# Gate rows by chunk and head on partitions, and the mLSTM units at other places in the order of the mixer stage

## The chip, the cores and the metric

The kernel runs on one core of a Trainium2 chip. The metric is the device time of one execution in microseconds (us). Three executions of the kernel before gave 1381.76, 1384.97 and 1388.18 us; the median is 1384.97 us. The profile belongs to one further execution.

Five engines work side by side, each through its own list of instructions, in order: PE multiplies matrices, DVE (VectorE) and ACT (ScalarE) work on tiles, POOL (GpSimd) is a third such engine, and SP issues DMA transfers. An instruction that waits holds up everything behind it on its engine, and nothing on the others unless they wait for it.

## The reference

The reference is one layer of a hybrid encoder over a prompt of 1024 frames and a running stream of 32 frames with a past of 256. The width is 1024. An adaptive norm modulates the input, one projection `w_in` feeds three groups of heads (mLSTM, forgetting attention "FoX", gMLP), one projection `w_o` joins them, then a norm, a SwiGLU FFN and a second norm follow. What the change touches is the gates:

```python
li = mi + b_mlstm_i                              # mLSTM input gate, 4 heads
lf = log_sigmoid(mf + b_mlstm_f)                 # mLSTM forget gate, 4 heads
logf = log_sigmoid(ff + b_fox_f)                 # FoX forget gate, 8 heads
# FoX: logits += F[t] - F[s],  F = cumsum(logf) over all frames
# mLSTM, chunk by chunk:
b = cumsum(lf)                                   # inside a chunk
m = maximum(m0 + b, max over s <= t of (b[t] - b[s] + li[s]))
m0_next = m[last]                                # and w = exp(... - m), d0 = exp(m0 + b[last] - m[last])
```

So the gates need cumulative sums over time, a running maximum of `li - b` inside each chunk, and a short recurrence over the chunks for the stabiliser `m0`. The kernel takes chunks of 128 frames: eight of the prompt and a ninth for the stream.

## The kernel before, in words

All matrices are split into a high and a low part of a reduced float32 type, so each step of a product is three matmuls: L117, L118 and L119 for products with features on partitions, L282, L283 and L284 for those with time on partitions (the stream's tile has L287, L288 and L290). A weight tile is loaded raw, ACT rounds it to its high part (L105), and DVE, or POOL where the order says so, subtracts to get the low part (L106). Every product's result comes in one of three PSUM banks `g`; transposes and small products share two banks `t`, attention scores two banks `s`, attention outputs one.

The stages are: the input and its modulation, the value projections (`tm_unit` v0 and v1, which also bring the gate columns), `gates()` (L424), then the mixer stage that the string `ORDER` lists, then the first four gMLP units and two key units, then `wo` (from 383 us in the profile), the norm, and the FFN with the rest of the mixers.

A token of `ORDER` is a unit: `q0` to `q7` the query and key product of a FoX head (`head_unit`, 24 matmuls of 512 columns; heads 0 and 1 have 48 more of 272 columns), `f0` to `f7` the attention of a head over the first 512 frames, in four tiles of 128 rows, `k0` and `k1` the key products of the mLSTM (a `p` puts L106 on POOL), `s` its states, `v` and `o` its value and output-gate products, `m0` to `m3` its first four chunks, and `a` one unit of the adaptive norm's modulation. An `a` unit loads two tiles `ada_late` of 512 KB, multiplies each in four matmuls (L179), has ACT copy the result, transposes it twice (L185), and DVE reduces it (L187).

The string isn't the final order. The program is built under a scheduler that simulates the engines with its own durations and writes a fixed list for each engine; units `f` and `m` are named with high priority. So a matmul of a later unit can fill a place at which the scheduler expects a wait. On the chip the lists are fixed: PE waits where its next instruction isn't ready. DMA transfers of SP are issued in its list's order, and a transfer that waits for its source or for a free tile holds those behind it.

`gates()` of before puts the four mLSTM heads and eight FoX heads in rows. It writes the gate columns into two tiles `gs` and `gl` of 96 columns a chunk, and for each of nine chunks multiplies by a triangle of ones (L464) and by the identity (L465), which gives `rb`: 96 rows (most of them empty) by nine chunks by 128 frames. The maximum is seven DVE steps over 4 rows by up to 1143 columns (L492), with POOL copying the start of each chunk (L493). The recurrence is three DVE steps a chunk (L504 to L506). FoX's cumulative sums get their carry (L471) and are split a chunk at a time (L475 to L478) and stored to DRAM `dfs`, from where `head_unit` loads four rows into `q2` and `k2`. Nine transposes of 128 by 128 (L530) and three DVE copies (L531) bring the results to columns `col`. The maximum goes to DRAM `dM`, from where each mLSTM chunk loads it, repeated over all partitions, into `mb`; DVE reads it in L585, the first step of a chunk.

A FoX tile's way is: two matmuls into a score bank (L752, L753), on DVE the mask on the diagonal (L755) and the row maximum (L756), on ACT the exponential (L761), on DVE the reciprocal (L765) and the scaling (L769), then transposes on PE (L788), a split on ACT and DVE (L794), and the products with the values (L796 to L805).

## Time and profile before

| what | before |
|---|---|
| median of the runs | 1384.97 us |
| profiled execution | 1386.62 us |
| its span, from first to last instruction | 1384.6 us |
| granted TensorE clock, mean | 0.99 |
| end of the value projections, PE | 106.95 us |
| `gates()` on PE | from 119.17 to 155.5 us |
| first attention score | 161.98 us |
| first matmul of `wo` | 383.24 us |

In the profile a row of a timeline gives the start and the duration of an instruction or of a group of like ones (`x8`), its engine, line and operation, the tiles out and in, and in brackets the idle time of that engine just before and what ended it. A row of windows gives for a stretch of time each engine's busy time, the TensorE clock that was granted (1.00 is full), the busy share of the DMA engines and GB/s. Matmuls overlap, so the time between the starts of two neighbours, and not their duration, is what one costs.

### The profile page before, as it was taken

How to read it: one execution, taken by the hardware profiler on the slowest of the kernel's cores; microseconds unless marked ns; L12 is line 12 of the kernel's file. 1: busy time of each engine (PE TensorE's matmuls, PEld its weight loads, DVE VectorE, ACT ScalarE, POOL GpSimd, SP SyncE). 2: the span in 40 equal slices, each digit the busy share in tenths (PEclk: the TensorE clock that was granted, in tenths of full speed). 3: DMA queues.
4: the chain of work that ended last, by engine and by line, in shares of the span. 5: the costliest groups of instructions: out<-in, count | busy, mean ns of one | idle time of the engine just before them, and what ended most of it. 6: DMA issues, size and time to landing. Idle time of an engine off the chain costs nothing.

```text
span 1384.6 us, 25402 instructions
## 1 busy us (share of the span) xinstructions
PE 1343.1 (97%) x9459; PEld 1226.1 (89%) x9459; DVE 1031.2 (74%) x2190; ACT 655.5 (47%) x1281; POOL 244.8 (18%) x276
## 2 busy tenths in 40 slices
PE   7999999999999899999999999999999999999996
PEld 4799788989899778888887889899999999999996
DVE  5547774678778757777776766678898988888777
ACT  3313354554545544545544455335564454545355
POOL 0102100042157500000000000264610000000341
PEclk9999999999999999999999999999999999999998
DMA  9763475455764765544444343564596768453321
GB/s 359 248 222 103 138 238 165 133 166 155 251 194 145 204 197 154 142 140 120 135 120 95 108 119 94 189 175 130 157 241 183 211 161 218 133 175 116 101 90 65
DMA packets 126386, 224.67 MB, mean 162 GB/s; under 512 B 21284, under 2 KB 70060, under 8 KB 126264
## 3 DMA queue, kind: packets, MB, share of 16 engines
q1 hardware_dynamic: 120952, 212.95, 49.4%
q0 software_dynamic: 5168, 9.96, 4.8%
q8 instruction: 75, 1.23, 0.4%
q14 instruction: 47, 0.39, 0.1%
q10 hardware_dynamic: 144, 0.14, 0.0%
HBM read 191.21 MB, written 51.72 MB: 175 GB/s over the span
## 4 chain that ended last, share of the span: by engine, by line
PE 83%; DVE 9%; DMA 4%; ACT 2%; issue 2%; POOL 1%; SPq 0%; DVEq 0%; ACTq 0%; POOLq 0%
PE up_g L117 5%; PE up_g L118 5%; PE up_g L119 5%; PE dn_g L119 4%; PE dn_g L117 4%; PE dn_g L118 4%; PE tm_g L282 3%; PE tm_g L283 3%; PE tm_g L284 3%; PE sup_u L119 3%; PE sup_u L117 3%; PE sup_u L118 3%; PE wo_g L118 2%; PE wo_g L119 2%; PE wo_g L117 2%; PE fox_t L788 2%
## 5 line engine op out<-in xcount | busy, mean ns | idle before, releaser
L117 PE MATMUL up_g<-mlstm_ah,up_whi 128*128 128x512 f32 (+1 forms) x384 | 141.3, 368 | 4.2 <-ACT lna_tmp L1037 3.4
L118 PE MATMUL up_g<-mlstm_al,up_whi 128*128 128x512 f32 (+1 forms) x384 | 141.5, 369 | 0.6 <-DVE mlstm_al L1042 0.6
L119 PE MATMUL up_g<-mlstm_ah,up_wlo 128*128 128x512 f32 (+1 forms) x384 | 140.7, 367 | 0.0
L283 PE MATMUL tm_g<-tm_wlo,start_h1h 128*128 128x256 f32 (+1 forms) x384 | 109.8, 287 | 0.0
L282 PE MATMUL tm_g<-tm_whi,start_h1h 128*128 128x256 f32 (+1 forms) x384 | 109.3, 287 | 0.0
L284 PE MATMUL tm_g<-tm_whi,start_h1l 128*128 128x256 f32 (+1 forms) x384 | 108.8, 285 | 0.0
L1161 ACT CAST sup_whi<-sup_raw 128x1024 fp32r<-128x1024 f32 x54 | 56.0, 1047 | 90.8 <-PE dn_u L118 47.4
L117 PEld LDWEIGHTS up_g<-mlstm_ah,up_whi 128*128 128x128 f32 x384 | 73.2, 191 | 16.9 <-ACT mlstm_ah L1041 3.6
L761 ACT ACTIVATE fox_p<-fox_s,fox_fmx 128x384 f32<-128x384 f32 (+2 forms) x96 | 55.2, 578 | 60.6 <-DVE fox_fmx L759 44.3
L118 PEld LDWEIGHTS up_g<-mlstm_al,up_whi 128*128 128x128 f32 x384 | 73.1, 190 | 11.9 <-DVE mlstm_al L1042 1.2
L119 PEld LDWEIGHTS up_g<-mlstm_ah,up_wlo 128*128 128x128 f32 x384 | 73.2, 191 | 10.6
L105 ACT CAST up_whi<-up_raw 128x1024 fp32r<-128x1024 f32 x50 | 52.4, 1048 | 61.6 <-PE up_g L118 18.2
L106 DVE TENSOR_TENSOR up_wlo<-up_raw,up_whi 128x1024 fp32r<-128x1024 f32 x50 | 66.8, 1336 | 14.0 <-ACT up_whi L105 13.3
L1016 DVE SCALAR_TENSOR_TENSOR wo_z<-dn_g,start_mod,wo_z 128x512 f32<-128x512 f32 (+4 forms) x120 | 60.2, 520 | 21.5 <-PE dn_g L119 19.6
L1162 DVE TENSOR_TENSOR sup_wlo<-sup_raw,sup_whi 128x1024 fp32r<-128x1024 f32 x54 | 68.1, 1264 | 10.5 <-ACT sup_whi L1161 10.5
L283 PEld LDWEIGHTS tm_g<-tm_wlo,start_h1h 128*128 128x128 f32 x384 | 72.3, 188 | 2.3 <-issue 2.1
L282 PEld LDWEIGHTS tm_g<-tm_whi,start_h1h 128*128 128x128 f32 x384 | 72.1, 189 | 1.7 <-issue 0.8
L117 PE MATMUL dn_g<-up_acth,dn_whi 128*128 128x512 f32 (+2 forms) x200 | 73.5, 368 | 0.0
L118 PE MATMUL dn_g<-up_actl,dn_whi 128*128 128x512 f32 (+2 forms) x200 | 73.4, 368 | 0.0
L119 PE MATMUL dn_g<-up_acth,dn_wlo 128*128 128x512 f32 (+2 forms) x200 | 73.3, 366 | 0.0
L284 PEld LDWEIGHTS tm_g<-tm_whi,start_h1l 128*128 128x128 f32 x384 | 72.2, 188 | 0.1
L117 PE MATMUL fm_g<-start_h1h,fm_whi 128*128 128x272 f32 (+2 forms) x200 | 60.6, 312 | 5.9 <-DVE fm_qkl L367 2.0
(628 smaller groups left out, 4628.9 us busy)
## 6 DMA issues: line engine op xcount, KB each, us to landing
up_raw<-w_gu SPq DMA_DIRECT2D x50, 512.0 KB
dn_raw<-w_dn SPq DMA_DIRECT2D x28, 512.0 KB
ada_late<-w_ada SPq DMA_DIRECT2D x24, 512.0 KB
wo_raw<-w_o SPq DMA_DIRECT2D x24, 512.0 KB
sup_raw<-w_gu SPq DMA_DIRECT2D x20, 512.0 KB
start_dp<-w_gu SPq DMA_DIRECT2D x19, 512.0 KB
start_dp<-w_gu POOLq DMA_DIRECT2D x19, 512.0 KB, 7.8
sup_raw<-start_dp SPq DMA_DIRECT2D x18, 512.0 KB
```

The source lines that it names most:

```text
L105: nc.scalar.copy(hi[:, :w], raw[:, :w])
L106: (eng or nc.vector).tensor_tensor(lo[:, :w], raw[:, :w], f(hi[:, :w]), ALU.subtract)
L117: nc.tensor.matmul(ps, hi, xh(k), start=start and k == 0, stop=False)
L118: nc.tensor.matmul(ps, hi, xl(k), start=False, stop=False)
L119: nc.tensor.matmul(ps, lo, xh(k), start=False, stop=stop and k == n - 1)
L282: nc.tensor.matmul(ps[:, :ncol], xh, hi, start=k == 0, stop=False)
L283: nc.tensor.matmul(ps[:, :ncol], xh, lo, start=False, stop=False)
L284: nc.tensor.matmul(ps[:, :ncol], xl, hi, start=False, stop=k == 7)
L761: nc.scalar.activation(pr[:, lo:hi], banks[x][:, :hi - lo], AF.Exp, bias=mxs[:, 0:1], accum_out=sums[:, x:x + 1])
L1016: self.lastz = self.nc.vector.scalar_tensor_tensor(z[:, m, x:y], ps[:, x - a:y - a], g[i], z[:, m, x:y], ALU.mult, ALU.add)
L1161: nc.scalar.copy(h, x)
L1162: tt(l, x, f(h), ALU.subtract)
```

## The change

Gates: a row is now a pair of chunk and head. The four gate tables are 36 or 72 columns wide, so one matmul for the FoX rows and three for the mLSTM rows replace the 18 of before. The maximum takes seven steps over 36 rows by 128 columns, shifted by a pad on the left. The carry of FoX's sums over the chunks is one small matmul with a matrix `ut` that POOL builds, and its split is done for all 64 rows at once; it is stored to `dfs` in two pieces. For the recurrence, the last column of each row is spread by a product with an indicator, one small matmul (`sel`) brings it to 4 heads by 18, eight DVE steps of 4 by 1 run the recurrence, and a second small matmul (`back`) brings `m0` and `m` back to the 36 rows. Four transposes of 36 rows and one copy give `col`. The pool of these tiles is on the other side of SBUF. `dfs` and `dM` have the new row order, so `decay()` loads four rows of `q2` or `k2` as four pieces of 512 bytes, and `mb` is one contiguous row of 2 KB for each partition.

Order: the mLSTM's key units, states and `v` come behind heads 0 and 1, `o` behind head 2, and chunks `m0` to `m3` in turns with heads 2 to 5.

```diff
-ORDER = "k0 k1p q0 f0 q1 a f1 s a q2 f2 a q3 f3 a v q4 f4 a q5 f5 o a m0 q6 f6 a m1 q7 m2 f7 a m3"
+ORDER = "q0 f0 q1 a f1 k0 k1p s a v q2 f2 a o a m0 q3 f3 a m1 q4 f4 a m2 q5 f5 a m3 q6 f6 a q7 f7"
...
+    def decay(self, out, h, rows, tiles):
+        j0, j1 = tiles
+        self.load(f(out).rearrange("p (j q) -> p j q", q=P),
+                  self.dfs.rearrange("(j h) r q -> h r j q", h=8)[h, rows, j0:j1])
...
-        self.load(f(q2[64:68]), self.dfs[h, 2:6, :512])
-        self.load(f(k2[64:68]), self.dfs[h, 0:4, :512])
+        self.decay(q2[64:68], h, slice(2, 6), (0, 4))
+        self.decay(k2[64:68], h, slice(0, 4), (0, 4))
...
-            for j in range(nj):
-                o = ps[:96, j * P:(j + 1) * P]
-                nc.tensor.matmul(o, gs[:, j0 + j, :], self.tri, start=True, stop=False)
-                nc.tensor.matmul(o, gl[:, j0 + j, :], self.ident, start=False, stop=True)
-            nc.scalar.copy(rb[:, j0:j0 + nj, :].rearrange("p j q -> p (j q)"), ps[:96, :nj * P])
...
+        ps = self.t(self.pt, [P, 512], F32, "t")
+        nc.tensor.matmul(ps[:72, 256:384], flat(gf), self.tri, start=True, stop=True)
+        nc.tensor.matmul(ps[:R, 0:128], flat(gn), self.tri, start=True, stop=False)
+        nc.tensor.matmul(ps[:R, 0:128], flat(gi), self.ident, start=False, stop=True)
+        nc.tensor.matmul(ps[:R, 128:256], flat(gm), self.tri, start=True, stop=True)
...
+        nc.tensor.matmul(pc[:64, 0:1], ut, rf[:64, P - 1:P], start=True, stop=True)
...
-            nc.vector.tensor_tensor(dst[:, :, w:], src[:, :, w:], src[:, :, :P - w], ALU.max)
-            nc.gpsimd.tensor_copy(dst[:, :, :w], src[:, :, :w])
...
+            nc.vector.tensor_tensor(v[:, 64:], u[:, 64:], u[:, w:w + P], ALU.max)
...
+        nc.tensor.matmul(pc[:4, 32:50], sel, EI.rearrange("p a j -> p (a j)"), start=True, stop=True)
+        ab = t([4, 2, 9], "ab")
+        nc.vector.tensor_copy(ab, pc[:4, 32:50].rearrange("p (a j) -> p a j", a=2))
         for j in range(8):
...
+            nc.vector.scalar_tensor_tensor(m0[:, j + 1:j + 2], ab[:, 0, j:j + 1], m0[:, j:j + 1], ab[:, 1, j:j + 1],
+                                           ALU.max, ALU.add)
+        nc.vector.tensor_copy(mm[:, 0, 0:8], m0[:, 0:8])
+        nc.vector.tensor_tensor(mm[:, 1, :], mm[:, 0, :], ab[:, 0, :], ALU.max)
+        nc.tensor.matmul(pc[:R, 64:82], back, mm.rearrange("p a j -> p (a j)"), start=True, stop=True)
...
-                nc.tensor.transpose(ps[:, j * P:(j + 1) * P], rs[:, j0 + j, :], self.ident)
...
+            nc.tensor.transpose(ps[:, R * g:R * g + R], rs[:, g, :], self.ident[:R, :R])
...
-        self.load(mb[:L, :, :L], self.dM[:, j, :L].partition_broadcast(L))
+        self.load(mb[:L, :, :L], self.dM[4 * j:4 * j + 4, :L].partition_broadcast(L))
```

Up to the end of the value projections PE's list is the same, and from `wo` on it is the same again but for line numbers. Three places show how the lists differ. `[waits ...]` names the engines and DMA queues that an instruction waits for.

In PE's list before, this stands behind the last transposes of the gates: the first `a` unit behind the gates (`ada_t_1496`) with a little of a key product (`fm_g`) inside, the first half of the next `a` unit, and the first scores of head 0.

```order
L179 MATMUL ada_t_1496<-ada_late_1497,start_c_63_182 32x256 [waits DMAHW7_49,DVE_49]
L179 MATMUL ada_t_1496<-ada_late_1497,start_c_63_182 32x256 x3
L179 MATMUL ada_t_1496<-ada_late_1503,start_c_63_182 32x256 [waits DMAHW0_49]
L179 MATMUL ada_t_1496<-ada_late_1503,start_c_63_182 32x256 x3
L117 MATMUL fm_g_2036<-start_h1h_171,fox_whi_1985 128x272
L118 MATMUL fm_g_2036<-start_h1l_172,fox_whi_1985 128x272
L119 MATMUL fm_g_2036<-start_h1h_171,fox_wlo_1986 128x272
L185 MATMUL ada_t_1496<-start_ident_121,ada_adas_1509 128x128 [waits Activation_49]
L185 MATMUL ada_t_1496<-start_ident_121,ada_adas_1509 128x128
L179 MATMUL ada_t_1518<-ada_late_1519,start_c_63_182 32x256 [waits DMAHW0_49,DVE_49]
L179 MATMUL ada_t_1518<-ada_late_1519,start_c_63_182 32x256 x3
L752 MATMUL fox_s_1904<-head_k_288_1785,head_qp_1787 128x128 [waits Activation_49]
```

In PE's list after, the same place begins at the end of head 1's first key product (`fm_g_1711`); `gates_t_1342` is the bank of the two small matmuls `sel` (L521) and `back` (L529).

```order
L119 MATMUL fm_g_1711<-start_h1h_171,fox_wlo_1661 128x272
L521 MATMUL gates_t_1342<-gates_EI_1366,gates_sel_1280 4x18 [waits DVE_49]
L529 MATMUL gates_t_1342<-gates_mm_1293,gates_back_1281 36x18 [waits DMAHW1_49,DVE_49]
L179 MATMUL ada_t_1407<-ada_late_1408,start_c_63_182 32x256 [waits DMAHW7_49,DVE_49]
L179 MATMUL ada_t_1407<-ada_late_1408,start_c_63_182 32x256 x3
L179 MATMUL ada_t_1407<-ada_late_1414,start_c_63_182 32x256 [waits DMAHW0_49]
L179 MATMUL ada_t_1407<-ada_late_1414,start_c_63_182 32x256 x3
L547 MATMUL gates_t_1399<-start_ident_121,gates_rs_1338 128x36 [waits DVE_49] x2
L547 MATMUL gates_t_1399<-start_ident_121,gates_rs_1338 128x36
L185 MATMUL ada_t_1407<-start_ident_121,ada_adas_1420 128x128 [waits Activation_49]
L185 MATMUL ada_t_1407<-start_ident_121,ada_adas_1420 128x128
L179 MATMUL ada_t_1429<-ada_late_1430,start_c_63_182 32x256 [waits DMAHW4_49,DVE_49]
```

The two small matmuls now stand back to back, the filling inside the first `a` unit is gone, and both halves of the next `a` unit (the second is `ada_late_1436`) stand ahead of the first scores.

In SP's list before, the load of the second `a` unit's tiles stands behind a FoX key's store, a weight and the decay rows of head 0.

```order
L91 DMA start_dql_58<-fm_qkl_1892 128x272 [waits DMAHW4_49,DVE_49]
L87 DMA tm_raw_2811<-w_in_f 128x1024 [waits DMAHW5_49]
L87 DMA head_q_291_1788<-start_dfs_64 4x512 [waits DMAHW6_49]
L87 DMA head_k_289_1786<-start_dfs_64 4x512 [waits DMAHW7_49,PE_49]
L87 DMA ada_late_1519<-w_ada 128x1024 [waits DMAHW0_49,PE_49]
L87 DMA ada_late_1525<-w_ada 128x1024 [waits PE_49]
```

In SP's list after, the same loads stand behind the stores of the gates' results.

```order
L91 DMA o_m<-gates_m_217_1291 4x1 [waits DMAHW0_49,DVE_49]
L91 DMA o_ms<-gates_mes_1393 4x1 [waits DMAHW1_49,DVE_49]
L91 DMA start_dd_11_67<-gates_d_244_1394 4x9 [waits DMAHW2_49,DVE_49]
L91 DMA start_dM_66<-gates_M_1386 36x128 [waits DMAHW3_49,DVE_49]
L87 DMA ada_late_1430<-w_ada 128x1024 [waits DMAHW4_49,PE_49]
L87 DMA fm_d0c_2127<-start_dd_11_67 64x2x9 [waits DMAHW5_49,DMAHW2_49]
L87 DMA ada_late_1436<-w_ada 128x1024 [waits DMAHW6_49,PE_49]
L87 DMA head_q_262_1463<-start_dfs_64 4x4x128 [waits DMAHW7_49]
L87 DMA head_k_260_1461<-start_dfs_64 4x4x128 [waits DMAHW0_49]
```

Four stores that wait for DVE's last gate results are now ahead of the `a` unit's loads, and the decay rows of head 0 are behind them.

In PE's list before, the scores of a late head (here head 7, `fox_s_3840` and `fox_s_3851` are its second and third tile) stand apart, with a gMLP product between.

```order
L752 MATMUL fox_s_3840<-head_k_701_3699,head_qp_3701 128x256 [waits DVE_49,PE_49]
L753 MATMUL fox_s_3840<-head_k_702_3700,head_q_704_3702 128x256
L282 MATMUL tm_g_4430<-tm_whi_4385,start_h1h_171 128x256
L283 MATMUL tm_g_4430<-tm_wlo_4386,start_h1h_171 128x256
L284 MATMUL tm_g_4430<-tm_whi_4385,start_h1l_172 128x256
L752 MATMUL fox_s_3851<-head_k_701_3699,head_qp_3701 128x384 [waits Activation_49]
L753 MATMUL fox_s_3851<-head_k_702_3700,head_q_704_3702 128x384
```

In PE's list after, the four tiles of head 4 stand together.

```order
L768 MATMUL fox_s_3213<-head_k_570_3163,head_qp_3165 128x128
L769 MATMUL fox_s_3213<-head_k_571_3164,head_q_573_3166 128x128 [waits DMAHW3_49]
L768 MATMUL fox_s_3224<-head_k_570_3163,head_qp_3165 128x256 [waits DVE_49,PE_49]
L769 MATMUL fox_s_3224<-head_k_571_3164,head_q_573_3166 128x256
L768 MATMUL fox_s_3235<-head_k_570_3163,head_qp_3165 128x384 [waits Activation_49]
L769 MATMUL fox_s_3235<-head_k_571_3164,head_q_573_3166 128x384
L768 MATMUL fox_s_3246<-head_k_570_3163,head_qp_3165 128x512 [waits Activation_49]
L769 MATMUL fox_s_3246<-head_k_571_3164,head_q_573_3166 128x512
L282 MATMUL tm_g_4013<-tm_whi_3962,start_h1h_169 128x256 [waits DVE_49]
```

Behind them come 24 matmuls of a gMLP product and four of the mLSTM, and then the transposes of all four tiles. On DVE, 26 instructions stand from the mask of the first tile to the scaling of the fourth: the 16 of the softmax and ten others. In the middle of the stage the query and key products of heads 3 to 7 now follow each other almost without a break (120 matmuls within 143 rows), and the first gMLP products run beside heads 3 to 7 and chunks `m1` to `m3`; before, they ran beside heads 6 and 7.

More of the change, by code (lines that the diff above doesn't have):

```diff
@@ L526, in gates @@
[L526 to L532 removed]
+        nc.vector.tensor_tensor(d0, mm[:, 0, :], mm[:, 1, :], ALU.subtract)
+        self.store(self.dd0, d0)
```

153 lines of the change are left out of this document (77 added, 76 removed).

## The prediction

> **What bounds the kernel now.** I read the page first, then a table of windows by stage, then PE's timeline inside the stage that the change reorders.
>
> ```profile
> PE 1343.1 (97%) x9459; PEld 1226.1 (89%) x9459; DVE 1031.2 (74%) x2190; ACT 655.5 (47%) x1281; POOL 244.8 (18%) x276
> PE 83%; DVE 9%; DMA 4%; ACT 2%; issue 2%; POOL 1%; SPq 0%; DVEq 0%; ACTq 0%; POOLq 0%
> ...
> 107.00:150.00 43.00, 43.00 (x319) 41.21 (x319) 35.31 (x101) 12.55 (x28) 11.06 (x17) 1.00 0.33 98
> 150.00:172.00 22.00, 18.66 (x121) 15.01 (x120) 13.02 (x30) 10.29 (x25) 1.70 (x3) 0.84 0.51 156
> 172.00:250.00 78.00, 77.92 (x566) 67.89 (x565) 46.16 (x120) 42.33 (x100) 2.99 (x4) 1.00 0.62 196
> 310.00:383.00 73.00, 68.78 (x544) 64.93 (x545) 56.72 (x169) 31.88 (x78) 17.22 (x22) 0.98 0.66 205
> 480.00:1384.00 904.00, 889.78 (x6017) 817.20 (x6015) 699.98 (x1362) 447.40 (x824) 129.35 (x131) 0.99 0.52 146
> ```
>
> PE is busy for 97% of the span and makes up 83% of the chain. In a row of windows the busy times of PE, weight loads, DVE, ACT and POOL follow the length, then the granted clock. From 107 to 150 us, where the gates run, PE is never idle, so what other engines do for the gates is hidden there: only PE's own instructions count, and waits. Two stretches of the reordered part lose time: 150 to 172 (3.34 us idle and a clock of 0.84) and 310 to 383 (4.22 us idle). Behind 383 the lists are equal; I take that part as unchanged. So the sum has three terms: PE's gate work, the waits of the first stretch, those of the second.
>
> **PE's gate work.** Before, on PE:
>
> ```profile
> 119.17 0.38 PE L464 MATMUL gates_t<-start_tri,gates_gs 128*96 128x128 f32 x2
> 119.39 0.38 PE L465 MATMUL gates_t<-start_ident,gates_gl 128*96 128x128 f32 x2
> ...
> 151.58 1.03 PE L530 MATMUL gates_t<-start_ident,gates_rs 128*128 128x128 f32 x8
> 152.99 0.39 PE L117 MATMUL fm_g<-start_h1h,fox_whi 128*128 128x272 f32 x1 [0.38 <-DVE fm_qkl L367]
> ...
> 157.72 0.44 PE L185 MATMUL ada_t<-start_ident,ada_adas 128*128 128x128 f32 x2 [0.15 <-ACT ada_adas L182]
> 160.97 1.08 PE L179 MATMUL ada_t<-ada_late,start_c 128*32 128x256 f32 x8 [2.81 <-DMA ada_late<-w_ada]
> 161.98 0.80 PE L752 MATMUL fox_s<-head_k,head_qp 128*128 128x128 f32 x2
> ```
>
> From 119.17 to 119.39 one product costs 0.22 us; 18 of them are 3.96. Eight transposes are 1.03 and a ninth about 0.12: together 5.1. After, there are four products of the same 128 columns (0.88), four transposes of a quarter of the columns and three matmuls of 1 to 18 columns. These seven have no row; between nothing and a full transpose (0.13) they are 0 to 0.9, and I take 0.6, nearer the transpose, since it is the smallest row of PE here. So 1.5 instead of 5.1: -3.6 us (ends -4.2 and -3.3). PE has no idle time to hide it in, so all of it shows.
>
> **DVE's and POOL's gate work.** DVE's groups by form from 107 to 157 us (count, busy us and mean ns at the end):
>
> ```profile
> L478 DVE TENSOR_SCALAR gates_fr<-gates_fr 8x256 fp32r<-8x256 f32 x8 | 2.3, 284 | 0.1
> L475 DVE TENSOR_SCALAR gates_ft<-gates_rb,gates_fc 8x128 f32<-8x128 f32 x8 | 2.2, 278 | 0.0
> L477 DVE TENSOR_TENSOR gates_fr<-gates_ft,gates_fr 8x128 fp32r<-8x128 f32 x8 | 2.2, 294 | 0.9 <-ACT gates_fr L476 0.8
> L504 DVE TENSOR_SCALAR gates_cm<-gates_cm,gates_m 4x128 f32<-4x128 f32 x7 | 1.9, 273 | 0.2
> L525 DVE TENSOR_TENSOR gates_rs<-gates_rb,gates_me 4x1152 f32<-4x1152 f32 x1 | 1.4, 1352 | 0.0
> L492 DVE TENSOR_TENSOR gates_cm<-gates_rb 4x1143 f32<-4x1143 f32 x1 | 1.3, 1339 | 0.0
> L506 DVE TENSOR_TENSOR gates_m<-gates_me,gates_gb 4x1 f32<-4x1 f32 x8 | 1.2, 147 | 0.2
> ```
>
> Time follows the columns and not the rows: 128 columns take 273 ns on 4 rows, 1143 take 1339. Seven scans of 128 columns therefore cost about 1.9 us instead of some 8.5, the split is done once (0.9) instead of eight times (6.7), and L504's seven and the wide copies go. DVE is about 15 us lighter. POOL loses its scan copies and gains seven small adds. I cost all this at nothing on the path: PE's other products, 43 us without idle time, cover it, and nothing in that stretch waits for DVE. What counts is only when the results are ready, next.
>
> **The waits of the first stretch.** In the changed list nothing stands between `sel` (L521) and `back` (L529). DVE does in that gap a copy, eight chained steps of 4 by 1, a copy and a maximum, 11 instructions at L506's 147 ns, 1.6 us, plus a hand-over each way (0.38 us stood idle at 152.99 behind a DVE instruction): PE idles 2.4 us where it ran a key product before. Then come eight `ada` matmuls, 1.08 us by the row at 160.97, beside the seven DVE steps (1.4 us) that the last transposes wait for: 0.3 idle. ACT's copy before L185: 0.4 (0.15 at 157.72, with three matmuls beside it that are gone). Then the next `ada_late`. The chain of waits has its transfer:
>
> ```profile
> 156.63 4.21 DMA ada_late<-w_ada
> ...
> 179.59 5.95 DMA mlstm_mb<-start_dM
> ```
>
> It is issued when the tile that it overwrites has been read, and lands 4.21 us later. Before, two head instructions, transposes and one key step lay beside it and 2.81 us were left. After, it is freed by the first half's four matmuls; the second half (0.5), the transposes (0.3), and the idle 0.7 lie beside it: 2.7 left, and with SP's four gate stores ahead of it and the fourth tile behind it, which the scores now stand behind too, 0.7 more. That makes 2.4 + 0.3 + 0.4 + 2.7 + 0.7 = 6.5 instead of 3.34: +3.2 us.
>
> The clock falls behind such a wait:
>
> ```profile
> 160.00:165.00 5.00, 4.03 (x21) 3.25 (x22) 2.27 (x8) 3.12 (x9) 0.54 (x1) 0.51 0.88 294
> 165.00:170.00 5.00, 5.00 (x34) 4.29 (x33) 2.48 (x8) 2.25 (x4) 1.16 (x3) 0.81 0.44 130
> ```
>
> Work at 0.51 and 0.81 loses 4.03 x 0.49 + 5 x 0.19 = 2.9 us. I take one such spell after as before, so no difference; ends: none (-2.9) or two (+2.9). The term is +3.2, from -6.2 (no waits, no spell) to +6.1.
>
> Here a rule of the Trainium skill speaks against my taking the spell as given. Its page "TensorE: Matmul & The Clock Gate", section "Part 1: The HAM clock gate (the "warmup" mystery)", says that the clock is halved after an idle window of about 3.4 us and restored after as long a busy one. By that, separate waits of 2.4 and 2.7 us with matmuls between would leave the clock up; that is the third rival below. The row above disagrees in part: 2.81 us idle was enough here.
>
> **The waits of the second stretch.** The two idle rows of before, two windows, DVE's softmax groups from 290 to 383 us, and what two neighbours of a gMLP-like product and two scores cost:
>
> ```profile
> 311.00 0.44 PE L598 MATMUL mlstm_t<-start_ident,mlstm_mqk 128*128 128x128 f32 x2 [2.20 <-DVE fox_ptl L794]
> 371.39 0.39 PE L117 MATMUL fm_g<-start_h1h,fm_whi 128*128 128x272 f32 x1 [1.98 <-DVE fm_qkl L367]
> ...
> 326.00:371.40 45.40, 42.85 (x349) 39.83 (x347) 41.86 (x131) 21.75 (x56) 9.44 (x12) 1.00 0.57 173
> 371.40:383.20 11.80, 11.80 (x82) 11.37 (x83) 4.14 (x9) 3.70 (x7) 2.52 (x4) 0.86 0.95 306
> ...
> L755 DVE TENSOR_TENSOR fox_s<-fox_s,start_maskneg 128x128 f32<-128x128 f32 x7 | 2.0, 288 | 0.0
> L756 DVE TENSOR_REDUCE fox_fmx<-fox_s 128x1 f32<-128x512 f32 x2 | 1.4, 680 | 0.0
> L769 DVE TENSOR_SCALAR fox_p<-fox_p,fox_fsm 128x512 f32<-128x512 f32 x2 | 1.3, 645 | 0.0
> L765 DVE RECIPROCAL fox_fsm<-fox_fsm 128x1 f32<-128x1 f32 x8 | 1.1, 150 | 0.0
> L769 DVE TENSOR_SCALAR fox_p<-fox_p,fox_fsm 128x128 f32<-128x128 f32 x2 | 0.6, 282 | 0.0
> L756 DVE TENSOR_REDUCE fox_fmx<-fox_s 128x1 f32<-128x128 f32 x2 | 0.6, 282 | 0.0
> ...
> 106.71 0.28 PE L287 MATMUL tm_g<-tm_wlo,start_hs 128*32 128x264 f32 x1
> 106.83 0.28 PE L288 MATMUL tm_g<-tm_whi,start_hs 128*64 128x264 f32 x1
> ...
> 168.42 0.33 PE L752 MATMUL fox_s<-head_k,head_qp 128*128 128x384 f32 x1
> 168.59 0.34 PE L753 MATMUL fox_s<-head_k,head_q 68*128 68x384 f32 x1
> ```
>
> From 326 to 371.4 DVE is busy for 92%: where gMLP products run beside heads 6 and 7, DVE is nearly the bound, and PE loses 2.55 us. In the changed list heads 3 to 7 run beside them. For head 4 the four tiles' scores stand together. DVE's softmax of them is four masks (1.15), four maxima from 0.282 to 0.680 (1.92), four reciprocals (0.60) and four scalings from 0.282 to 0.645 (1.85), 5.5 us, with ten other DVE instructions between at no less than 0.15 each: 7.0. PE has seven more scores (0.17 each, 1.2), 24 gMLP matmuls (0.12 each, 2.9) and four small ones (0.11, 0.4) until it needs the fourth tile: 4.5. So it waits 2.5, with hand-overs 3. For head 5 the same count gives DVE 5.5 + 15 x 0.15 = 7.8 and PE 66 rows, 7.9: 1 us by hand-overs. Against that, the wait of 2.20 at 311.00 stood at a place that no longer exists; I let it go. The wait at 371.39 stands in front of the key units, whose neighbours are the same, and stays. So 3 + 1 - 2.2 = +1.8. Lower end: no new waits, and those at 311.00 and 371.39 go with the clock's loss behind the latter (11.80 x 0.14 = 1.7): -5.9. The upper end is DVE as the bound, in the second rival: +13.6.
>
> **The small ones.** `mb` lands 5.95 us after its issue; now a partition reads one row of 2 KB instead of four of 512 bytes. Its reader stands in DVE's list ahead of a score's maximum, as before. I take 0 (-1 to +2). The four pieces for a decay row are 0, counted above as late only with the queue. Between head 7's end and `wo` there remain 116 PE rows, some 14 us, under which `wo`'s last operands are loaded: 0 (up to +3).
>
> **Sum.** -3.6 + 3.2 + 1.8 = +1.4 us on the profiled execution's 1386.62, so 1388.0. That execution lies 1.65 above the median of the runs; on the median, 1386.4 us. What the gates give PE is taken back by two small matmuls that wait for each other and by softmaxes that come too soon. Changes under 0.5% (6.9 us) can hardly be told from none.
>
> **Rivals.**
> Faster: the lighter DVE decides. Its results come early, the waits of the first stretch and their spell vanish (-6.2), head 4's wait doesn't come and 311.00 goes (-2.2): -3.6 - 6.2 - 2.2 = -12.0, 1373 us. For it speaks that DVE has 35.31 of 43 us busy where the gates are, and loses 15. Against it: `back` cannot start before DVE's chain behind `sel`, and the `ada` load isn't DVE's. It decides once the first stretch idles under 2 us.
> Slower: DVE as the bound of the second stretch. Adding mean durations over DVE's list gives 45.0 us for the part that took 45.40, and 89.3 for the changed list from the first gMLP product beside head 3 to the end of `m3`; PE's rows there are 77.5. At the same busy share of 92% these take 97 and lose 19.5, where the stretch from 310 on lost 5.9 (4.22 idle, 1.7 clock): +13.6 instead of +1.8, so 1398 us. At full use of DVE, 11.8 are lost, +5.9, and 1390.5. It decides once DVE is used for less than 98% there.
> Clock up: the waits come as I say but without a spell: 2.9 less, 1383.5. One row at 0.51 after 2.81 us speaks against it, the 2.20 at 311.00 without a fall of the clock for it.
>
> **Chances.** My forecast 0.38 and the clock kept up 0.10 both lie within 0.5% of before: 0.48. Faster 0.22. Slower 0.30, since a region twice as long at DVE's limit is easier to reach than a first stretch without waits. The range goes from 1372 to 1399: the lower end reaches the faster case's time, the upper that of the slower. For the likeliest alone it is 1380 to 1392.
>
> **What would show it.** Right: PE's gate rows add up to some 1.5 us; idle rows of about 2.4 at L529 and 3 at L179 close to each other, with a clock near 0.5 behind; an idle row of some 3 us at head 4's transposes (L804), put down to DVE's scaling L785. Wrong: PE idle under 2 us before the first score (the faster case), or DVE over 90% busy and PE idle by over 10 us between the first gMLP product and `wo` (the slower one).

## The result and the profile after

The changed kernel takes 1394.78 us (median of 14 runs, 1390.12 to 1401.42), the kernel before 1385.62 us in as many runs beside it (1381.76 to 1388.43). The ratio is 1.006, with a 95% interval of 1.0047 to 1.0072: slower by 0.6%, 9.2 us. That is inside the range of the prediction (1372 to 1399), but outside the 1380 to 1392 that it gave for its likeliest case, which was no change that can be told from none. One execution of a later kernel, before_fp, took 2181.32 us at a granted clock of 0.56 and is left out of that kernel's median and ratio.

The page of the changed kernel begins so; its profiled execution took 1401.42 us, the slowest of its runs:

```profile
span 1398.5 us, 25229 instructions
PE 1346.6 (96%) x9432; PEld 1227.3 (88%) x9432; DVE 1006.3 (72%) x2144; ACT 655.4 (47%) x1274; POOL 235.7 (17%) x269
```

DVE is lighter by 25 us over the whole span, and the kernel is slower all the same. The same windows as before show where the time went (columns as before: PE, weight loads, DVE, ACT, POOL, then the clock):

```profile
107.00:150.00 43.00, 35.00 (x225) 29.24 (x224) 25.23 (x94) 14.15 (x34) 5.58 (x8) 0.84 0.48 137
150.00:172.00 22.00, 20.50 (x171) 19.14 (x170) 12.44 (x33) 9.41 (x24) 0.92 (x2) 1.00 0.62 205
172.00:250.00 78.00, 78.00 (x617) 72.47 (x617) 24.50 (x59) 26.57 (x59) 2.00 (x3) 1.00 0.45 137
250.00:310.00 60.00, 55.26 (x341) 46.34 (x340) 43.62 (x123) 34.21 (x74) 10.62 (x14) 0.97 0.57 161
310.00:383.00 73.00, 71.21 (x579) 67.04 (x578) 56.96 (x175) 36.44 (x91) 16.06 (x17) 0.98 0.50 149
480.00:1384.00 904.00, 898.03 (x6066) 823.54 (x6064) 698.07 (x1360) 443.56 (x817) 131.49 (x137) 0.99 0.52 147
```

The stretch from 107 to 150 us, which had no idle PE before, now has 8 us of it; 250 to 310 has 4.7. PE's idle rows, with the first matmul of `wo` at 391.67 (383.24 before) and the first `up` behind the norm at 475.61 (466.16 before):

```profile
129.48 0.24 PE L529 MATMUL gates_t<-gates_mm,gates_back 4*36 4x18 f32 x2 [2.47 <-DVE gates_mm L528]
134.99 1.08 PE L179 MATMUL ada_t<-ada_late,start_c 128*32 128x256 f32 x8 [2.75 <-DVE start_mod L197]
138.57 1.08 PE L179 MATMUL ada_t<-ada_late,start_c 128*32 128x256 f32 x8 [2.50 <-DMA ada_late<-w_ada]
164.63 0.33 PE L812 MATMUL fox_o<-fox_ptl,head_v 128*64 128x256 f32 x1 [1.50 <-DVE fox_ptl L810]
286.12 0.36 PE L768 MATMUL fox_s<-head_k,head_qp 128*128 128x256 f32 x1 [1.33 <-DVE fm_C L644]
287.97 0.44 PE L768 MATMUL fox_s<-head_k,head_qp 128*128 128x384 f32 x1 [1.37 <-ACT fox_p L777]
295.68 0.44 PE L685 MATMUL mlstm_t<-start_ident,mlstm_mhm 128*128 128x128 f32 x2 [1.03 <-DVE mlstm_mhm L675]
313.86 0.44 PE L768 MATMUL fox_s<-head_k,head_qp 128*128 128x384 f32 x1 [1.18 <-ACT fox_p L777]
386.01 0.40 PE L117 MATMUL fm_g<-start_h1h,fm_whi 128*128 128x272 f32 x1 [2.02 <-DVE fm_qkl L367]
391.67 0.38 PE L117 MATMUL wo_g<-fox_ah,wo_whi 128*128 128x256 f32 x1 [1.06 <-ACT tm_gms L719]
475.61 0.36 PE L117 MATMUL up_g<-fox_ah,up_whi 128*128 128x256 f32 x1 [3.35 <-ACT lna_tmp L1053]
```

And the clock beside the first three:

```profile
130.00:135.00 5.00, 2.23 (x23) 1.06 (x25) 4.24 (x14) 2.92 (x7) 0.64 (x2) 0.65 0.51 119
135.00:140.00 5.00, 2.50 (x18) 0.80 (x19) 0.66 (x1) 3.03 (x7) 0.00 (x0) 0.50 0.68 221
140.00:145.00 5.00, 5.00 (x24) 5.00 (x24) 2.88 (x9) 1.86 (x7) 1.70 (x3) 0.50 0.61 160
```

In finer windows the clock is 1.00 from 129.5 to 131.5, 0.50 in every window from 131.5 to 145, and 0.97 from 145 to 148. So it fell behind the first wait, before the second and the third, and stayed down for some 13.5 us.

The row at 134.99 names DVE's L197, but L179 reads nothing that L197 writes. The trace's semaphore records have the landing of its `ada_late` at 134.85, and L179 starts 3.92 us after the issue of that transfer (131.07). So I read the wait as one for the transfer, as the prediction had it.

Two windows up to `wo` give the balance, of before and then of after:

```profile
107.00:162.00 55.00, 51.66 (x385) 47.31 (x384) 42.02 (x114) 17.94 (x41) 11.06 (x17) 0.98 0.38 113
162.00:383.24 221.24, 215.73 (x1611) 194.51 (x1609) 150.74 (x416) 109.52 (x261) 35.50 (x42) 0.98 0.59 184
```

```profile
107.00:139.60 32.60, 24.60 (x164) 18.98 (x162) 18.47 (x72) 8.87 (x20) 3.03 (x3) 0.88 0.42 123
139.60:391.67 252.07, 240.97 (x1796) 220.31 (x1792) 149.13 (x416) 116.33 (x270) 33.86 (x41) 0.97 0.54 163
```

Up to the first score PE idles 8.0 us instead of 3.3, and from there to `wo` 11.1 instead of 5.5: 10.3 us more. PE's busy time there falls by 1.8. Three things add up in it: the gates give PE less to do, more of the work runs at a low clock, and the changed kernel is 2.4 us further on in its list when these windows begin. Together that is the shift of 8.4 us at `wo`, and with 1 us more of the norm 9.45 at the first `up`, close to the 9.2 us of the medians.

The 2.4 us come from ahead of the gates, where PE's list is the same: the value projections end at 104.57 us instead of 106.95. Most of it is a wait of before at 47 us. Rows of before, and then DVE's row of after:

```profile
43.87 2.51 DVE L217 TENSOR_SCALAR ada_h<-ada_x,start_mod 128x1024 f32<-128x1024 f32 x1
44.26 0.81 POOL L452 MEMSET gates_gs<- 128x864 f32 x1
47.08 0.94 PE L117 MATMUL fm_g<-start_h1h,fm_whi 128*128 128x512 f32 x3 [1.40 <-ACT start_h1h L222]
```

```profile
42.80 1.00 DVE L217 TENSOR_SCALAR ada_h<-ada_x,start_mod 128x1024 f32<-128x1024 f32 x1
```

Before, POOL clears the two wide gate tables `gs` and `gl` while DVE modulates the input (L217), which takes 2.51 us, and PE stands for 1.40 us behind it. The new gates don't have these tables; the same instruction takes 1.00, and the wait is gone. All three kernels with the old gates have 2.50 or 2.51 there, all eleven with the new ones 0.80 to 1.00. That it is POOL's work which slows DVE is inferred from the overlap; no run takes the one away alone. The other 0.6 us lies ahead of 22 us and differs between kernels with the same list there.

What the profiled execution is longer by beyond the 9.45 us lies behind 480 us. One execution of each kernel is profiled, so whether that part is chance can't be told. Below I compare places by the time of the first `up` (rows with the 3.3 us wait for `lna_tmp`) and kernels by their medians.

### The profile page after: what moved, and what is told of

Its sections match the earlier page's. It is cut to its first block, busy times and chain, and to the rows that moved or that the text cites. A ratio compares the mean times of both kernels' runs of the same rounds, so it can differ in the third digit from the quotient of the medians.

```text
span 1398.5 us, 25229 instructions
## 1 busy us (share of the span) xinstructions
PE 1346.6 (96%) x9432; PEld 1227.3 (88%) x9432; DVE 1006.3 (72%) x2144; ACT 655.4 (47%) x1274; POOL 235.7 (17%) x269
## 4 chain that ended last, share of the span: by engine, by line
PE 63%; DVE 5%; DMA 2%; issue 1%; ACT 1%; POOL 0%; SPq 0%; DVEq 0%; ACTq 0%
PE up_g L117 5%; PE up_g L118 5%; PE up_g L119 5%; PE dn_g L117 4%; PE dn_g L119 4%; PE dn_g L118 4%; PE sup_u L117 2%; PE sup_u L119 2%; PE sup_u L118 2%; PE wo_g L117 2%; PE wo_g L118 2%; PE wo_g L119 2%; PE sup_g L119 2%; PE sup_g L118 2%; PE sup_g L117 2%; PE fox_t L804 2%
## 5 line engine op out<-in xcount | busy, mean ns | idle before, releaser
L117 PE MATMUL up_g<-fox_ah,up_whi 128*128 128x512 f32 (+1 forms) x384 | 142.0, 370 | 4.7 <-ACT lna_tmp L1053 3.3
L118 PE MATMUL up_g<-fox_al,up_whi 128*128 128x512 f32 (+1 forms) x384 | 142.5, 371 | 0.6 <-DVE fox_al L1058 0.6
L119 PE MATMUL up_g<-fox_ah,up_wlo 128*128 128x512 f32 (+1 forms) x384 | 141.3, 368 | 0.0
L117 PEld LDWEIGHTS up_g<-fox_ah,up_whi 128*128 128x128 f32 x384 | 73.5, 192 | 17.4 <-ACT fox_ah L1057 3.5
L118 PEld LDWEIGHTS up_g<-fox_al,up_whi 128*128 128x128 f32 x384 | 73.6, 192 | 12.4 <-DVE up_actl L1111 0.8
L119 PEld LDWEIGHTS up_g<-fox_ah,up_wlo 128*128 128x128 f32 x384 | 73.8, 192 | 10.8
L1178 DVE TENSOR_TENSOR sup_wlo<-sup_raw,sup_whi 128x1024 fp32r<-128x1024 f32 x54 | 68.0, 1262 | 10.8 <-ACT sup_whi L1177 10.8
L106 DVE TENSOR_TENSOR up_wlo<-up_raw,up_whi 128x1024 fp32r<-128x1024 f32 x50 | 66.6, 1332 | 10.3 <-ACT up_whi L105 9.6
L105 ACT CAST dn_whi<-dn_raw 128x1024 fp32r<-128x1024 f32 (+1 forms) x44 | 42.7, 971 | 48.3 <-PE up_g L118 11.4
```

The source lines that it names most:

```text
L105: nc.scalar.copy(hi[:, :w], raw[:, :w])
L106: (eng or nc.vector).tensor_tensor(lo[:, :w], raw[:, :w], f(hi[:, :w]), ALU.subtract)
L117: nc.tensor.matmul(ps, hi, xh(k), start=start and k == 0, stop=False)
L118: nc.tensor.matmul(ps, hi, xl(k), start=False, stop=False)
L119: nc.tensor.matmul(ps, lo, xh(k), start=False, stop=stop and k == n - 1)
L1178: tt(l, x, f(h), ALU.subtract)
```

## The experiments

**The two halves apart.** Theory A: the order string loses, by where it puts the units. Rival B: the new gates lose wherever the units stand. Four kernels: the gates alone, the string alone, and the new gates with the front or the tail of the new string.

```diff
 # gates_only: the changed kernel with the string of before
+ORDER = "k0 k1p q0 f0 q1 a f1 s a q2 f2 a q3 f3 a v q4 f4 a q5 f5 o a m0 q6 f6 a m1 q7 m2 f7 a m3"
 # order_only: the kernel before with the new string
+ORDER = "q0 f0 q1 a f1 k0 k1p s a v q2 f2 a o a m0 q3 f3 a m1 q4 f4 a m2 q5 f5 a m3 q6 f6 a q7 f7"
 # front_moved: the changed kernel, new front, tail of before
+ORDER = "q0 f0 q1 a f1 k0 k1p s a q2 f2 a q3 f3 a v q4 f4 a q5 f5 o a m0 q6 f6 a m1 q7 m2 f7 a m3"
 # tail_moved: the changed kernel, front of before, new tail
+ORDER = "k0 k1p q0 f0 q1 a f1 s a v q2 f2 a o a m0 q3 f3 a m1 q4 f4 a m2 q5 f5 a m3 q6 f6 a q7 f7"
```

> The new gates with the order string of before. In PE's list 44 instructions then stand between the two small matmuls L521 and L529, and between the scores of a head and its transposes at least as much as before. Theory A (the change loses by its order string: the waits of the first stretch and of heads 4 and 5 come from the places of the units): the gates alone save their PE time, 3.6 us, and add no wait, so 1379 to 1383 us, ratio to before about 0.997; idle at L529 under 0.3 us. Rival B (the new gates themselves lose, since two small matmuls wait for DVE wherever they stand, and the decay rows come in small pieces): the wait of about 2.5 us at L529 and those at L179 are there again with a clock near 0.5 behind them, and the time is 1388 us or more.

> The gates of before with the new order string. Theory A: the late stretch loses as in the changed kernel (6.4 us idle at heads 4 and 5 and some 2.7 us more by the clock than before), and the first stretch is free of the wait at L529, which this kernel doesn't have: 1390 to 1395 us, ratio about 1.005. Rival B: the order string costs nothing by itself, 1384 to 1388 us.

> The new gates, with the new places of the mLSTM key units behind heads 0 and 1, and from there the order of before. Theory A: the first stretch loses as in the changed kernel (8 us idle instead of 3.3, and a clock spell of 4.6 instead of 2.9 us, against 3.6 us of PE work saved), the late stretch as before: about +2.8, 1387 to 1390 us. Rival (the first stretch's waits are made up later, since PE would have waited there anyway): 1383 to 1386 us.

> The new gates, the mLSTM key units at the start as before, and from the units v and o on the new order. Theory A: no wait in the first stretch (3.6 us saved), the late stretch loses nearly as in the changed kernel (+6 to +8): 1387 to 1391 us. Rival (the late waits follow from what the first stretch leaves behind on DVE and go with it): 1380 to 1383 us.

| kernel | gates | front | tail | median, us | ratio to before | first `up` in its profile |
|---|---|---|---|---|---|---|
| before | old | old | old | 1385.07 | | 466.16 |
| gates_only | new | old | old | 1377.13 | 0.9945 (0.9929 to 0.9961) | 461.83 |
| front_moved | new | new | old | 1387.25 | 1.0015 (1.0004 to 1.0026) | 468.47 |
| tail_moved | new | old | new | 1390.64 | 1.0039 (1.0025 to 1.0053) | 469.89 |
| after | new | new | new | 1394.78 | 1.006 (1.0047 to 1.0072) | 475.61 |
| order_only | old | new | new | 1418.3 | 1.0239 (1.0220 to 1.0258) | |

Theory A holds: the gates alone make the kernel faster, and the string takes it back and more. The gates give more than theory A's 3.6 us: 2.8 of the 4.3 us at the first `up` are there at the end of the value projections (104.18 instead of 106.95). The front and the tail cost 6.6 and 8.1 us at the first `up`, together 13.8: nearly their sum. By the medians it isn't so: they cost 10.1 and 13.5, and together 17.7, less than their sum. What neither theory had is order_only, 33 us slower. Its PE row:

```profile
154.58 2.15 PE L530 MATMUL gates_t<-start_ident,gates_rs 128*128 128x128 f32 x9 [23.47 <-DVE gates_rs L525]
```

The gates' DVE work of before runs until 154 us, and the key products of the mLSTM were what PE did meanwhile. Without them ahead, PE stands for 23.5 us and then works at half clock. So the gates' shorter way through DVE is worth a lot, but only with the new string; with the old one PE had work beside it, as the prediction had it. front_moved shows the same three rows as the changed kernel, so these come from the front alone:

```profile
129.37 0.24 PE L529 MATMUL gates_t<-gates_mm,gates_back 4*36 4x18 f32 x2 [2.47 <-DVE gates_mm L528]
134.85 1.08 PE L179 MATMUL ada_t<-ada_late,start_c 128*32 128x256 f32 x8 [2.73 <-DVE start_mod L197]
139.13 1.08 PE L179 MATMUL ada_t<-ada_late,start_c 128*32 128x256 f32 x8 [3.20 <-DMA ada_late<-w_ada]
```

tail_moved has none of them. Its waits are at head 4, behind it, and in the middle of `wo`:

```profile
274.70 0.36 PE L768 MATMUL fox_s<-head_k,head_qp 128*128 128x256 f32 x1 [1.32 <-DVE fox_C L644]
276.54 0.44 PE L768 MATMUL fox_s<-head_k,head_qp 128*128 128x384 f32 x1 [1.37 <-ACT fox_p L777]
297.97 0.44 PE L614 MATMUL mlstm_t<-start_ident,mlstm_mqk 128*128 128x128 f32 x2 [4.26 <-DVE fox_ptl L810]
386.26 0.58 PE L117 MATMUL wo_g<-fox_ah,wo_whi 128*128 128x256 f32 x1 [5.03 <-DVE fm_qkl L367]
```

**The `a` units of the first stretch.** The changed kernel with the two `a` units that stand behind the gates named ahead of them:

```diff
-T1 = (1, 1, 0, 2)
+T1 = (1, 1, 2, 0)
```

> The changed kernel with the two a units that stand behind the gates named ahead of them. In PE's list 17 matmuls of a key product (some 2.1 us) then stand between L521 and L529, and no L179 between the gates and the first scores. Theory A (the first stretch loses by its own three waits and the clock spell that they bring): of the 8 us idle between the gates and the first score under 3 are left and the clock stays up, so 6 to 10 us less than the changed kernel: 1385 to 1389 us. Rival (the waits only move: the a units wait for their loads ahead of the gates, or PE waits for the decay rows instead): 1392 us or more.

Measured: 1389.6 us, ratio 1.0023 (1.0011 to 1.0036), 5.2 us less than the changed kernel; the first `up` comes at 468.34, 7.3 earlier. Of the 8 us idle 4.6 are left, in other rows, and a clock spell with them:

```profile
132.09 0.51 PE L547 MATMUL gates_t<-start_ident,gates_rs 36*128 36x36 f32 x3 [1.30 <-DVE gates_rs L535]
135.87 0.79 PE L768 MATMUL fox_s<-head_k,head_qp 128*128 128x128 f32 x2 [3.26 <-ACT head_k L403]
```

The second is a wait for head 0's keys (L403), and ACT's own rows tell where it is from: ACT stands for 6.81 us for the gates' last copy, with the head's work behind it in its list.

```profile
132.98 0.29 ACT L549 ACTIVATE start_col<-start_col 128x108 f32<-128x108 f32 x1 [6.81 <-DVE start_col L548]
135.23 0.58 ACT L403 CAST head_k<-head_g 64x512 fp32r<-64x512 f32 x1
```

The result is between theory and rival: the waits at L529 and L179 were real and are gone, but about half of what they cost is taken up by head 0's preparation, which was late as well.

**Is DVE the limit of the late stretch?** The prediction's slower case had DVE as the bound there, and the prediction's own wait was for DVE's scaling (L785). The switch `FP` moves this scaling to ACT for the first 512 frames:

```diff
-FP = (0, 0)
+FP = (1, 0)
```

> The changed kernel with the scaling of the probabilities (L785, 1.7 us for the four tiles of a head) on ACT instead of DVE for the first 512 frames. Theory D (DVE is what heads 4 and 5 wait for): DVE has 14 us less to do, the idle rows of heads 4 and 5 (6.4 us together) fall below 3, and the time is 1388 to 1391 us. Rival S (the scores wait for one of their two PSUM banks, that is for mask, maximum and exponential of the tile two before, wherever the scaling is): the same idle rows at L768 stay over 5 us, ACT's exponential comes later, and the time is 1394 us or more.

> The new gates with the order of before, and the scaling on ACT as above. Theory D: the late idle rows of the new gates with the order of before (303.59, 343.30 and 365.62, 4.5 us together) shrink, 1373 to 1376 us. Rival S: no gain, 1377 us or more.

> The kernel before with the scaling on ACT. It tells how much of the 14 us of the new gates with that scaling (1372 against 1386) is the scaling's: if the two add up, the new gates give 8 and the scaling 5 to 6, so 1379 to 1382 us here; if the scaling helps only with the new gates, 1384 us or more.

| kernel | median, us | ratio to before |
|---|---|---|
| after_fp | 1400.49 | 1.0102 (1.0085 to 1.0119) |
| gates_fp | 1371.93 | 0.9891 (0.9873 to 0.9909) |
| before_fp | 1387.17 | 1.0007 (0.9992 to 1.0023) |

In the changed kernel it loses 6 us more, with head 4's rows no smaller, new ones further on, and a longer wait in `wo`:

```profile
285.51 0.36 PE L768 MATMUL fox_s<-head_k,head_qp 128*128 128x256 f32 x1 [1.73 <-DVE fm_C L644]
287.48 0.69 PE L768 MATMUL fox_s<-head_k,head_qp 128*128 128x384 f32 x1 [1.49 <-ACT fox_p L777]
299.60 0.44 PE L804 MATMUL fox_t<-start_ident,fox_p 128*128 128x128 f32 x2 [1.30 <-ACT fox_p L783]
397.34 0.58 PE L117 MATMUL wo_g<-fox_ah,wo_whi 128*128 128x256 f32 x1 [3.79 <-DVE fm_qkl L367]
```

So theory D falls for the changed kernel: from 280 to 320 us DVE is busy for 36.10 of 40 us in the changed kernel and for 32.27 here, and head 4's waits are no shorter. Rival S has the time right and not the rows: head 5's two at L768 (1.18 and 0.61) are gone, and 1.30 at L804 and 1.83 at L685 (316.60) have come. The waits stand at the scores, and the scores wait for a bank: the second score of head 4 for the bank that DVE's state update of the chunk (L644) still reads, the third for the exponential of the first tile. In DVE's timeline of the changed kernel, the four steps of that update stand between the chunk's other steps and the first mask, without a gap:

```profile
284.82 1.16 DVE L644 SCALAR_TENSOR_TENSOR fm_C<-fm_C,fm_d0c,mlstm_s 64x65 f32<-64x65 f32 x4
286.01 0.68 DVE L824 TENSOR_TENSOR fox_fo<-fox_o,fox_fo 64x512 f32<-64x512 f32 x1
286.62 0.28 DVE L771 TENSOR_TENSOR fox_s<-fox_s,start_maskneg 128x128 f32<-128x128 f32 x1
```

With the new gates and the old string the scaling on ACT gains 5.2 us (1377.13 to 1371.93; by their ratios, each to the runs of before beside it, it is 7), with the old gates nothing. Theory D named three late rows of that string, 4.5 us together: the first is 1.31 instead of 1.36, the second is gone, the third is 0.55 instead of 2.33. So there the late waits did shrink, though not all that ends them is DVE's (the third row ends with ACT). The time is below theory D's, since a wait of the first stretch is gone as well, which the next experiment looks at.

**The transfer of `mb`.** The new gates with the old string wait once in the first stretch. PE's row, and DVE's at the same place:

```profile
161.96 0.69 PE L804 MATMUL fox_t<-start_ident,fox_p 128*128 128x128 f32 x2 [2.65 <-DMA start_dql<-head_k]
```

```profile
160.89 0.61 DVE L601 SCALAR_TENSOR_TENSOR mlstm_mw<-mlstm_mb,start_col,start_maskbig 128x128 f32<-128x128 f32 x2 [5.17 <-issue]
161.42 0.48 DVE L785 TENSOR_SCALAR fox_p<-fox_p,fox_fsm 128x512 f32<-128x512 f32 x1
```

DVE stands for 5.17 us ahead of L601, and head 0's last scaling, for which the transposes wait, stands behind it. gates_mb loads `mb` ahead of its neighbours:

```diff
         t = lambda shape, tag, bufs=1: self.t(mx, shape, F32, tag, bufs)
+        mb = t([P, 4, P], "mb", 1)
+        self.load(mb[:L, :, :L], self.dM[4 * j:4 * j + 4, :L].partition_broadcast(L))
         qk = t([P, 4, P], "mqk", 1)
...
-        mb = t([P, 4, P], "mb", 1)
-        self.load(mb[:L, :, :L], self.dM[4 * j:4 * j + 4, :L].partition_broadcast(L))
```

> The new gates with the order of before, and the load of mb named ahead of the loads of mqk and mqb, so that it is issued some 4 us earlier. Theory M (DVE's idle time of 5.17 us ahead of L601, behind which head 0's last scaling stands, is the transfer of mb, and PE's wait of 2.65 us at 161.96 follows from it): PE's wait and its clock spell go, 1372 to 1375 us. Rival: DVE waits there for something else, PE's wait stays above 2 us, 1377 us.

Measured: 1389.91 us, ratio 1.0019 (1.0007 to 1.0031), 13 us slower than gates_only (10 by the ratios). The time that theory M gave is missed. At the place itself theory M holds: PE's wait is 0.76 instead of 2.65, and the clock stays at 1.00.

```profile
161.24 0.50 PE L768 MATMUL fox_s<-head_k,head_qp 128*128 128x128 f32 x2 [0.76 <-ACT head_k L403]
```

But 70 us later both kernels are at the same point (a score of head 3 at 232.15 and 232.19), and the first `up` comes only 0.9 earlier (460.93). Of this, 1.3 us were lost ahead of the edit: the value projections of this execution end at 105.48 instead of 104.18. For the rest no idle row tells why. The edit also changed the scheduler's list far behind it, down to the second part of `wo`, where PE waits 2.7 us for ACT that gates_only doesn't. That wait doesn't make 10 to 13 us; the rest stays open. gates_fp goes the other way round the same wait: there the scaling isn't on DVE, so it can't stand behind L601, and the row at 161.96 and its clock spell are gone. The score of head 3 comes at 228.70, 3.5 us earlier than in gates_only. Before, `mb` was waited for too (3.03 us on DVE at 185.57), but PE has no idle row behind it, and before_fp gains nothing.

**What of the tail costs.** vo_early has the new gates, the front of before, `v` and `o` early, but the chunks late as before:

```diff
+ORDER = "k0 k1p q0 f0 q1 a f1 s a v q2 f2 a o q3 f3 a q4 f4 a q5 f5 a m0 q6 f6 a m1 q7 m2 f7 a m3"
```

> The new gates, the mLSTM key units at the start as before, the units v and o at their new early places, but the chunks m0 to m3 where they were, beside heads 6 and 7. It stands between the new gates with the order of before (1377) and the kernel with v, o and the chunks moved (1391). Theory T (the chunks in turns with heads 2 to 5 make the loss: a chunk's state update, a gMLP norm and a head's scores meet on DVE and in the two score banks): the idle rows at L768 behind L644 vanish, 1377 to 1382 us. Rival V (v and o early make it: they run with no attention beside them, and the gMLP products are left for the end): 1387 us or more.

Measured: 1391.23 us, ratio 1.0040 (1.0026 to 1.0055). The rows at L768 are gone, as theory T has it, and yet the time is rival V's, since PE now waits at `wo`:

```profile
379.78 1.01 PE L117 MATMUL wo_g<-mlstm_ah,wo_whi 128*128 128x256 f32 x3 [9.39 <-ACT mlstm_ah L983]
```

It waits 9.4 us for an operand's high part that ACT makes, and ACT itself waits for the operand, the last chunk's output, which has gone to DRAM and is loaded from there:

```profile
379.11 3.91 ACT L983 CAST mlstm_ah<-mlstm_al 128x512 fp32r<-128x512 f32 x6 [7.66 <-DMA mlstm_al<-start_dmix]
```

With `v` and `o` early, the gMLP products come earlier too (the last of their mixing products, L709, at 345.66 us; in gates_only at 373.37), and none are left to cover the way from the last chunk to `wo`. So the chunks in turns aren't the whole of it. I read the two kernels so: early `v` and `o` spend the filler, and where the chunks stand decides whether the loss shows at the scores or at `wo`.

after_s3 asked the bank directly, with three score banks and two for products:

```diff
-NB = (3, 2, 2)
+NB = (2, 2, 3)
```

> The changed kernel with three score banks and two banks for products instead of two and three. If the bank is what heads 4 and 5 wait for (rival S), the idle rows of 1.2 to 1.4 us ahead of their second and third scores (L768) go. The time says less, since products lose a bank: 1390 us if only the scores had waited, 1396 us or more if DVE's softmax is the next thing to wait for, which would show as idle rows at L804.

Measured: 1425.19 us, ratio 1.0284 (1.0265 to 1.0304). It doesn't settle the question. The second score no longer waits, but the third and fourth do, and products wait all over the late stretch, as at 374.20:

```profile
287.97 0.41 PE L768 MATMUL fox_s<-head_k,head_qp 128*128 128x384 f32 x1 [1.35 <-DVE fm_C L644]
289.48 0.80 PE L768 MATMUL fox_s<-head_k,head_qp 128*128 128x512 f32 x1 [0.93 <-ACT fox_p L777]
374.20 0.38 PE L282 MATMUL tm_g<-tm_whi,start_h1h 128*128 128x256 f32 x1 [3.73 <-DVE tm_tmres L297]
```

The wait for DVE's state update moved on by one score with the third bank: that speaks clearly for the bank as what holds the score up; what the wait is worth in time isn't shown.

**The better kernel once more.** gates_fp with the `a` units early as well:

```diff
-T1 = (1, 1, 0, 2)
+T1 = (1, 1, 2, 0)
```

> The new gates with the order of before and the scaling on ACT, and the two a units ahead of the gates. In the changed kernel that saved 5 us, but there three waits of the first stretch were to be had. With the order of before and the scaling on ACT this stretch has no idle row over 0.1 us, so there is nothing to gain: 1371 to 1374 us; a gain below 1369 would mean that PE loses time there that no idle row shows.

Measured: 1375.83 us, ratio 0.9928 (0.9911 to 0.9946), 4 us slower than gates_fp and 2 us above what I expected: a wait of 1.86 us for ACT comes in at 162.37. gates_fp, with 1371.93 us and a ratio of 0.9891, beats both kernels of this case by 14 and 23 us.

## Why the prediction was right or wrong

**That PE's own gate work and the waits decide, and the rest is hidden:** right for the old string from 107 us on; gates_only keeps PE busy through the gates. It was read from the old string's windows, though, and order_only shows how much that cover is worth: 23.5 us. It is wrong ahead of the gates: POOL's and DVE's gate work was put at nothing, and at 47 us a wait of 1.40 us goes with POOL's two clearings.

**The waits of the first stretch (+3.2, with no difference in the clock):** the mechanism was right and its rows are there, the size was too small. L529 waits 2.47 us against 2.4. The step that failed is the second `ada_late`: I had 2.7 and 0.7 for its two halves, and they wait 2.75 and 2.50, since the second half's transfer is issued 1.15 us behind the first half's and takes 6.3 us instead of 4.21. (Before, the two were issued 0.43 us apart, at 156.63 and 157.06, and no wait stands between the halves.) Idle is up by 4.7. The clock's spell is longer than before: 2.23 x 0.35 + 2.50 x 0.50 + 5 x 0.50 = 4.5 us lost against 2.9 (4.1 by the finer windows). So the term is +6.3 and not +3.2. The Trainium skill's rule on the clock ("TensorE: Matmul & The Clock Gate", "Part 1: The HAM clock gate (the "warmup" mystery)"), by which separate waits under 3.4 us would leave the clock up, doesn't hold in this trace: no wait is longer than 2.75 us, and the clock is at 0.50 for some 13.5 us. The rival that rested on it falls.

**The waits of the second stretch (+1.8):** this step failed in kind and in size. I priced PE's transposes waiting for DVE's scaling. The waits are at the scores, ahead of all of the softmax, for a bank that the mLSTM's state update holds and for the exponential of the tile two before. I had counted DVE's instructions from the first mask on, as if the scores could be written at once, though there are two score banks for four tiles. From the first score to `wo` idle is up by 5.6 us (1.5 of it is `mb`'s, next), and the clock loses some 2.5 us more. The sign that the prediction named, an idle row at head 4's transposes (L804) put down to L785, didn't come. The wait at 311.00 went, as I had it, and the one at 371.39 came again (2.02 at 386.01).

**`mb` (0, from -1 to +2):** too low, but inside its own bounds. In the changed kernel DVE waits 3.38 us for it, and PE 1.50 behind that (164.63).

**The faster rival** needed an idle time under 2 us in the first stretch; it was 8. **The slower rival** had the right sign and the wrong reason: from the first gMLP product beside head 3 (276 us) to `wo` DVE is busy for 90.44 of 115.67 us, 78%, and PE idles 9.6 us; the prediction asked for over 90% and over 10. It is nearer its limit than this mean says only from 280 to 320 us (36.10 of 40), where the waits of heads 4 and 5 stand. Taking the scalings away from it (10 us less busy over the span) made the kernel slower.

**Luck:** the upper end of the range, 1399, is the slower rival's time. Without that rival the range would have ended at 1392, and 1394.78 would have lain outside it. So the range held by a mechanism that didn't happen.

**The sum:** gates -3.6, first stretch +6.3, second +8.1, together +10.8; the shift at `wo` is 8.4 and at the first `up` 9.45. The difference is the term that the prediction didn't have, -2.4 us ahead of the gates: with it the sum is 8.4. It closes better than its terms are known: adding up, for each gate instruction of PE, the time until it ends or the next one starts gives 4.8 us before and 2.4 after, so the gates' own term may be -2.4 and not -3.6, and PE's records aren't complete.

## What to carry to other kernels

A change that makes a chain shorter is worth what the chain stood in the way of, and that depends on the work that is placed beside it: here the same gates are worth 8 us in one order and 24 in another. Filler is a stock: a product that fills a place early isn't there at the end, so an order string should be judged by the last join (here `wo`) as well as by the place it mends. When several tiles share two banks, count the wait from the bank: from the reader of the tile two before, and from what stands ahead of that reader in its engine's list. Look at the stretches that a change shouldn't touch as well: 2.4 us of this one came 60 us ahead of the gates. And a scheduler that writes the lists anew can change the time by 10 us for one moved line (gates_mb), so a few us between two strings don't tell of one unit without the rows beside them.

## What was unexpected in the hardware

The clock fell to 0.50 some 2 us behind a wait of 2.47 us and stayed there for some 13.5 us, in which two more waits of 2.75 and 2.50 us lie. A wait of 2.20 us before (311.00) was followed by 1.00, and the windows with and behind one of 4.26 us in tail_moved (297.97) have 0.86 and 0.80: the length of a single wait doesn't tell the clock's answer. Two transfers of 512 KB that were issued 1.15 us apart (131.07 and 132.22) were waited for until 134.99 and 138.57, 3.9 and 6.3 us after their issue. A DVE instruction of 128 by 1024 took 2.51 us with POOL's clearings beside it and 1.00 without them. And the profiled execution of a kernel can lie at an end of its runs: here it is the slowest of 14, and of the 13.9 us by which its span is longer than before's, 4.5 lie behind the first `up`, where PE's lists of the two are alike.
